# A two-layer decoder trunk on one core: the turned planes are joined on ScalarE, a token half at a time

## The chip, the core and the metric

The kernel runs on one core of one Trainium2 chip. TensorE (PE in the rows) multiplies, VectorE (DVE) and ScalarE (ACT) do the elementwise work, SyncE (SP) issues most transfers, and each engine takes its instructions strictly in the order in which they are written. The metric is the device time of one execution in microseconds (us), the median of several runs.

## What is computed

256 tokens of width 2048 pass through two layers. Each layer has one input projection, a main branch (layer 0: trailing-window means; layer 1: block attention with shared keys and values, which for 256 tokens is plain causal attention), a memory branch (4 heads over 256 memory tokens), gates, one output projection and a layer norm:

```python
for i in range(2):
    if i == 1: k, v = split(h @ w_kv_shared)              # 12 heads of 128
    branch_in, gate_b, mem_q, gate_m = split(h @ w_in[i]) # 1536, 1536, 512, 512 columns
    branch = multiscale_pool(branch_in) if i == 0 else causal_attention(branch_in, k, v)
    mem_o = memory_attention(mem_q, mem, w_mem_kv[i])
    mixed = concat(branch * silu(gate_b), mem_o * silu(gate_m))
    h = layer_norm(ALPHA * h + mixed @ w_out[i])
```

All of it is float32. Each operand of a product is held as a high and a low part, and three products are summed: high by high, high by low, low by high.

## The kernel before

**Items and blocks.** All weights come as items of 128x1024 numbers (512 KB), in a list that is walked once by `run()` (L135). One turn of its loop is called a block here. In block i the program writes, in this order: the preparation of item i+3 (`LP`: ScalarE copies `raw` into the high part `wh`, VectorE subtracts to get the low part `wl`, L73 and L74), the load of item i+4 (`LD`, on SyncE's queue), the matmuls of item i (12 of 512 columns for a projection whose tokens are stationary), and then whatever functions `later(n, fn)` has put down for this block. `raw`, `wh` and `wl` have four buffers each, so item i+3 can be prepared only when TensorE has finished item i-1. Eight items make one projection of 512 columns (`proj_n`, L209); its two token halves t=0 and t=1 end in the last item, the second half as much later as half an item takes.

**Turned projections.** Queries, keys, gates and the pooled input are wanted with channels on the partitions. `turned()` (L260) does that: ScalarE splits the result into planes of high and low 16-bit halves (L265, one instruction a token half), SyncE sends each token half as a DMA transpose (L268), and `join` (L286) puts the halves together again into 32-bit numbers, by VectorE copies of 16-bit numbers (L291) that write every second half-word. For `heads` (queries and keys) ScalarE then makes the high part (L298) and VectorE the low part one block later (L299); for `gates` (which first go through tanh, L276, and L277) and `to_pool` the joined numbers are the result. There are 9 projections for heads, 8 for gates and 3 for the pool.

**Distances.** They are counted in blocks after the last item i of the projection: sends in block i+4 (`SEND`), the join of both halves and the high part in block i+4 (`JOIN`), the low part in block i+5, for gates two blocks later for the join and one for the send. `plan(pr, a, turns, b, c)` (L471) does so for the attention of a pair of heads, counted from the last item of the query projection: scores in block `a` (6 for the first pair, 13 for the second), exponentials and division one and two later, the VectorE transposes in `turns`, the split of the probabilities in `b` and b+1, and the output, gate and split into `zT` in `c`. Nothing else sets an order: there is no scheduler.

**Order of layer 1.** Memory keys, memory values, memory queries (8 items each), memory gates, and then three groups of 32 items: keys, queries, gates, values. The first group's query projection ends 24 blocks after the memory queries. The output projection (`out_proj`, L700) ends with 16 items j8 to j23, after every second of which a kept item (one that is prepared here and multiplied after the loop) stands. `load_gb_rows` (L769) prepares four pieces of the last norm's constants (`split_rows`, L780: one ScalarE and two VectorE instructions each), in the blocks 9 to 12 after the output projection's first item.

Of the kernel before, what the change touches and what calls it, by code (L numbers as in the profile page):

```python
# [18 lines left out]
P = 128  # L19
# [23 lines left out]
LP = 3  # L43
SEND = 4
JOIN = 4
# [4 lines left out]
def trunk(ctx: ExitStack, tc: tile.TileContext, a: dict, out: bass.AP):  # L50
# [43 lines left out]
    def later(n, fn):  # L94
        events[now[0] + n].append(fn)
# [164 lines left out]
    def turned(where, then, gate=False):  # L260
# [9 lines left out]
        def done(t, acc):  # L270
# [10 lines left out]
            later(SEND + gate, lambda: send(t))  # L281
            if t == 1:
                later(JOIN + GATE * gate, lambda: then([tp.rearrange("p (h n) t -> p n h t", h=2) for tp in tps], pls[0]))
        return done

    def join(dst, tps, n0=0):  # L286

        n = dst.shape[1]
        to = dst.bitcast(U16).rearrange("p n (t h) -> p n h t", h=2)
        for t, tp in enumerate(tps):  # L290
            nc.vector.tensor_copy(to[:, :, :, t * P:(t + 1) * P], tp[:, n0:n0 + n])  # L291

    def heads(dst, where):
        def then(tps, pl):
            whole = pl.rearrange("p t h n -> p (t h n)").bitcast(F32).rearrange("p (n t) -> p n t", t=T)
            hi, lo = dst()[:, :, :T], dst()[:, :, T:]
            join(whole, tps)
            nc.scalar.activation(hi, whole, AF.Copy)  # L298
            later(1, lambda: nc.vector.tensor_sub(lo, whole, f(hi)))  # L299
        return turned(where, then)  # L300

    def gates(slots, where):
        def then(tps, pl):
            n0 = 0
            while n0 < 4:
                n = 1
                while n0 + n < 4 and slots[n0 + n] == slots[n0] + n:
                    n += 1
                join(gate[:, slots[n0]:slots[n0] + n], tps, n0)
                n0 += n  # L310
        return turned(where, then, gate=True)
# [273 lines left out]
    def mem_q_gate(layer):  # L585
# [5 lines left out]
        def go():  # L591
            plan(prs[0], 6, (9, 10, 11, 11), 12, 15)
            plan(prs[1], 13, (16, 18, 21, 23), 25, 28)
        after(go)
# [23 lines left out]
    items += [rest[0], xs[3]] + rest[1:]  # L618
    after(lambda: later(JOIN + GATE + 1, pools))

# [21 lines left out]
    def to_pool(base):  # L642
        def then(tps, pl):
            i = base
            while i < base + 4:
                n = min(3 - i % 3, base + 4 - i)
                join((U0, U1)[i // 3 % 2][:, i % 3:i % 3 + n, PAD:], tps, i - base)
                i += n
                if i % 3 == 0:
                    for j, fn in enumerate(pool_group(i // 3 - 1)):  # L650
                        n = (j + 1) // 2 + 4 * (i == 12)
                        if n:
                            later(n, fn)
                        else:
                            fn()
        return turned(in_q, then)
# [53 lines left out]
    for c in range(3):  # L710
        weave(collect(proj_n, xT, cols(a["w_in"][0], c), to_pool(4 * c)), mixes, 5)
        items += mixes
        proj_n(xT, cols(a["w_in"][0], 3 + c), gates([(4 * c + d + 4) % SLOTS for d in range(4)], in_q))
        mixes = sum((collect(pool_mix, g) for g in ((0,), (1,), (2, 3))[c]), [])
    after(lambda: later(4, load_x))

    weave(out_proj(0, range(4)), mixes, 5)

# [32 lines left out]
    for grp in range(3):  # L751
# [7 lines left out]
        def go(prs=prs, grp=grp):  # L759
            plan(prs[0], 6, (9, 10, 10, 11), 12, 19)  # L760
            plan(prs[1], 13, (16, 18, 19, 21), 23, 25)
        after(go)
# [6 lines left out]
    def load_gb_rows():  # L769
# [7 lines left out]
        for n in range(4):  # L777
            later(9 + n, lambda n=n: split_rows(f(raw)[:, n * 512:(n + 1) * 512], n))

# [174 lines left out]
```

## Time and profile before

| | us |
|---|---|
| median of 3 runs | 812.81 (812.37 to 814.1) |
| profiled execution, device time | 813.08 |
| its span, first to last instruction | 811.1 |
| TensorE busy | 798.5 (98%) |
| VectorE busy | 604.5 (75%) |
| ScalarE busy | 411.0 (51%) |

Busy time of TensorE is the union of its matmuls, each of which is drawn longer than the distance to the next one, so a pause shows in full only in the distance between two starts.

### The profile page before, as it was taken

Reading aid. Unit: us, or ns where it says so; the run is one execution under the profiler, and the core shown is the slowest. Engines: PE = TensorE matmul, PEld = TensorE weight load, DVE = VectorE, ACT = ScalarE, POOL = GpSimd, SP = SyncE. Lnnn points to the kernel's source line nnn. Section 1 sums busy time; section 2 is a strip of 40 time slices with the busy share of each in tenths; the row PEclk is TensorE's granted clock in tenths of the full one; section 3 lists DMA queues with packets and bytes.
Section 4 is the critical chain, followed back from the end, with each engine's and each line's share of the span. In section 5 each row is a group of like instructions: output and inputs, shape, how many; then the busy total and the mean of one; then the engine's idle time right before and its main releaser. Section 6 shows DMA issues by size and latency. Waiting matters only on the chain.

```text
span 811.1 us, 10158 instructions
## 1 busy us (share of the span) xinstructions
PE 798.5 (98%) x3724; PEld 664.2 (82%) x3724; DVE 604.5 (75%) x841; ACT 411.0 (51%) x523; POOL 0.2 (0%) x4
## 2 busy tenths in 40 slices
PE   9999999999999999999999998999999999999997
PEld 6888888888888888888888877888888888887786
DVE  5684699867687765687459777986589756997847
ACT  5555544655554443455455556545555655555520
POOL 0000000000000000000000000000000000000000
PEclk9999999999999999999999999999999999999999
DMA  8877777787777766686676775657765776656742
GB/s 302 289 239 245 204 187 201 187 224 219 214 228 272 252 192 192 192 279 199 197 207 176 163 215 178 204 184 208 218 187 181 200 223 197 196 183 209 268 146 104
DMA packets 110022, 169.53 MB, mean 209 GB/s; under 512 B 47632, under 2 KB 49680, under 8 KB 109712
## 3 DMA queue, kind: packets, MB, share of 16 engines
q1 hardware_dynamic: 108656, 165.70, 67.8%
q10 hardware_dynamic: 1316, 3.19, 1.1%
q8 instruction: 29, 0.48, 0.3%
q14 instruction: 21, 0.16, 0.1%
HBM read 156.28 MB, written 2.10 MB: 195 GB/s over the span
## 4 chain that ended last, share of the span: by engine, by line
PE 86%; DVE 7%; issue 2%; DMA 2%; ACT 2%; SPq 0%; DVEq 0%; ACTq 0%
PE acc L69 79%; PE s L69 3%; DVE wl L74 2%; PE o L69 2%; PE pt L69 2%; DVE p L361 1%; DMA raw<-in_w_in 1%; ACT wh L73 1%; DMA raw<-in_w_mk 1%; DVE xm L74 0%; DMA ln_g<-pl 0%; ACT ebuf L337 0%; DMA raw<-in_w_out 0%; SPq L268 0%; DVE res L488 0%
## 5 line engine op out<-in xcount | busy, mean ns | idle before, releaser
L69 PE MATMUL acc<-wh,xm 128*128 128x512 f32 x1344 | 421.4, 391 | 0.0
L74 DVE TENSOR_TENSOR wl<-raw,wh 128x1024 fp32r<-128x1024 f32 (+4 forms) x250 | 293.9, 1186 | 142.2 <-ACT wh L73 140.9
L73 ACT ACTIVATE wh<-raw 128x1024 fp32r<-128x1024 f32 (+4 forms) x250 | 254.0, 1027 | 190.9 <-PE acc L69 125.7
L69 PEld LDWEIGHTS acc<-wh,xm 128*128 128x128 f32 x1344 | 253.1, 188 | 52.3
L69 PE MATMUL acc<-wl,xm 128*128 128x512 f32 x672 | 262.6, 391 | 1.0 <-DVE wl L74 1.0
L69 PEld LDWEIGHTS acc<-wl,xm 128*128 128x128 f32 x672 | 126.7, 188 | 27.1 <-DVE wl L74 1.8
L69 PE MATMUL acc<-wh,zT 128*128 128x512 f32 x448 | 139.4, 390 | 0.0
L69 PEld LDWEIGHTS acc<-wh,zT 128*128 128x128 f32 x448 | 84.1, 188 | 17.3
L69 PE MATMUL acc<-wl,zT 128*128 128x512 f32 x224 | 87.7, 392 | 1.3 <-DVE wl L74 1.3
L69 PE MATMUL acc<-xm 128*128 128x512 f32 x288 | 66.3, 389 | 0.0
L361 DVE STREAM_TRANSPOSE p<-ebuf 32x192 f32<-32x192 f32 (+1 forms) x160 | 63.3, 396 | 2.4
L69 PEld LDWEIGHTS acc<-xm 128*128 128x128 f32 x288 | 53.9, 188 | 11.0
L74 DVE TENSOR_TENSOR xm<-raw,xm 128x1024 fp32r<-128x1024 f32 (+2 forms) x41 | 47.9, 1169 | 13.5 <-ACT xm L73 13.0
L69 PEld LDWEIGHTS acc<-wl,zT 128*128 128x128 f32 x224 | 42.1, 188 | 11.4 <-DVE wl L74 3.0
L73 ACT ACTIVATE xm<-raw 128x1024 fp32r<-128x1024 f32 (+2 forms) x41 | 41.1, 1010 | 16.6 <-DMA raw<-in_w_out 5.2
L265 ACT ACTIVATE pl<-acc 128x1024 uint16<-128x1024 uint16 x24 | 23.9, 1018 | 5.1 <-PE acc L69 4.3
L69 PE MATMUL acc<-xm,wh 128*128 128x512 f32 x64 | 24.3, 421 | 0.8 <-ACT wh L73 0.8
L69 PE MATMUL acc<-xm,zT 128*128 128x256 f32 (+1 forms) x144 | 22.6, 318 | 0.0
L337 ACT ACTIVATE ebuf<-p,nb 128x128 f32<-128x128 f32 (+1 forms) x24 | 10.7, 445 | 23.3 <-DVE nb L333 23.3
L73 ACT ACTIVATE pp<-p 128x384 fp32r<-128x384 f32 (+1 forms) x20 | 11.2, 559 | 22.1 <-DVE p L361 22.1
L69 PEld LDWEIGHTS acc<-xm,zT 128*128 128x128 f32 x144 | 20.7, 190 | 1.9
L73 ACT ACTIVATE zT<-zf 128x512 fp32r<-128x512 f32 (+1 forms) x18 | 10.5, 581 | 22.2 <-DVE zf L367 17.5
(137 smaller groups left out, 518.8 us busy)
## 6 DMA issues: line engine op xcount, KB each, us to landing
raw<-in_w_in SPq DMA_DIRECT2D x128, 512.0 KB, 4.9
raw<-in_w_out SPq DMA_DIRECT2D x64, 512.0 KB, 4.2
raw<-in_w_sk SPq DMA_DIRECT2D x24, 512.0 KB, 4.7
raw<-in_w_sv SPq DMA_DIRECT2D x24, 512.0 KB, 3.4
raw<-in_w_mv SPq DMA_DIRECT2D x14, 512.0 KB, 5.4
raw<-in_w_mk SPq DMA_DIRECT2D x12, 512.0 KB, 5.0
raw<-in_xT SPq DMA_DIRECT2D x4, 512.0 KB, 5.4
res<-in_x ACTq DMA_DIRECT2D x2, 1024.0 KB, 6.5
```

The source lines that it names most:

```text
L69: nc.tensor.matmul(o, l, r, start=start, stop=stop, **kw)
L73: nc.scalar.activation(hi, src, AF.Copy)
L74: nc.vector.tensor_sub(lo, src, f(hi))
L265: nc.scalar.activation(pls[0][:, t], src.bitcast(U16).rearrange("p (n h) -> p h n", h=2), AF.Copy)
L337: nc.scalar.activation(dst, src, AF.Exp, bias=self.nb[:, c:c + 1], scale=SCALE, accum_out=self.sm[:, c:c + 1])
L361: nc.vector.transpose(self.p[32 * g:32 * g + 32, h * self.n:(h + 1) * self.n], self.e[32 * h:32 * h + 32, g * self.n:(g + 1) * self.n])
```

## The change

The join moves from VectorE to ScalarE, as a copy by `activation`, and is done for each token half by itself: the half t in block i+4+t. For `heads` the joined half goes into the part of the `pl` tile that the same half's planes came from. To make room the sends move a block forward (`SEND` 3), the scores of all pairs and everything behind them a block back (the memory pairs' second output two: 28 to 30), the high part to block i+5 and the low part to i+6; the steps of the pool start a block after the second half's join; the woven items of the pool's mixing stand one place later, and so does the load of `x`. `split_rows` moves from 9 to 12 blocks after the output projection's first item to 31 to 34 blocks after it, which is the loop's last block and behind it.

```diff
-SEND = 4
+SEND = 3
 JOIN = 4
@@ turned
             later(SEND + gate, lambda: send(t))
+            tp = tps[t].rearrange("p (h n) x -> p n h x", h=2)
+            later(JOIN + t + GATE * gate, lambda: then(t, tp, pls[0]))
-            if t == 1:
-                later(JOIN + GATE * gate, lambda: then([...both halves...], pls[0]))
@@ join
-    def join(dst, tps, n0=0):
-        n = dst.shape[1]
-        to = dst.bitcast(U16).rearrange("p n (t h) -> p n h t", h=2)
-        for t, tp in enumerate(tps):
-            nc.vector.tensor_copy(to[:, :, :, t * P:(t + 1) * P], tp[:, n0:n0 + n])
+    def join(dst, tp, n0=0):
+        n = dst.shape[1]
+        nc.scalar.activation(dst.bitcast(U16).rearrange("p n (x h) -> p n h x", h=2), tp[:, n0:n0 + n], AF.Copy)
@@ heads
-        def then(tps, pl):
-            whole = pl.rearrange("p t h n -> p (t h n)").bitcast(F32).rearrange("p (n t) -> p n t", t=T)
-            hi, lo = dst()[:, :, :T], dst()[:, :, T:]
-            join(whole, tps)
-            nc.scalar.activation(hi, whole, AF.Copy)
-            later(1, lambda: nc.vector.tensor_sub(lo, whole, f(hi)))
+        def then(t, tp, pl):
+            whole = pl.rearrange("p t h n -> p (t h n)").bitcast(F32).rearrange("p (t n x) -> p n t x", t=2, n=4)
+            join(whole[:, :, t], tp)
+            if t == 1:
+                hi, lo = (dst()[:, :, c:c + T].rearrange("p n (t x) -> p n t x", t=2) for c in (0, T))
+                nc.scalar.activation(hi, whole, AF.Copy)
+                later(1, lambda: nc.vector.tensor_sub(lo, whole, f(hi)))
@@ gates, to_pool: the same join, for the columns t * P:(t + 1) * P alone
@@ mem_q_gate
-            plan(prs[0], 6, (9, 10, 11, 11), 12, 15)
-            plan(prs[1], 13, (16, 18, 21, 23), 25, 28)
+            plan(prs[0], 7, (10, 11, 12, 12), 13, 16)
+            plan(prs[1], 14, (17, 19, 22, 24), 26, 30)
@@ the pool
-    after(lambda: later(JOIN + GATE + 1, pools))
+    after(lambda: later(JOIN + GATE + 2, pools))
-                        n = (j + 1) // 2 + 4 * (i == 12)       (n = 0: at once)
+                        later(1 + j // 2 + 3 * (i == 12), fn)   (behind the second half)
@@ the lists: weave(..., mixes, 5) becomes 6, twice; later(4, load_x) becomes 5
@@ the three groups of layer 1
-            plan(prs[0], 6, (9, 10, 10, 11), 12, 19)
-            plan(prs[1], 13, (16, 18, 19, 21), 23, 25)
+            plan(prs[0], 7, (10, 11, 11, 12), 13, 20)
+            plan(prs[1], 14, (17, 19, 20, 22), 24, 26)
@@ load_gb_rows
-            later(9 + n, lambda n=n: split_rows(f(raw)[:, n * 512:(n + 1) * 512], n))
+            later(31 + n, lambda n=n: split_rows(f(raw)[:, n * 512:(n + 1) * 512], n))
```

What stands on the engines, at three places. First VectorE, before the change, where the memory branch of layer 1 ends and the first group's queries come in: the second memory pair's output (`zf` from `o`), its split into `zT`, the join of the queries, their low part, and the masking of the first group's scores (`p` from `s`).

```order
L74 TENSOR_TENSOR wl<-raw,wh 128x1024 x2
L367 SCALAR_TENSOR_TENSOR zf<-o,gate 128x512
L74 TENSOR_TENSOR zT<-zf,zT 128x2x256
L291 COPY pl<-ln_g 128x4x2x128 x2
L74 TENSOR_TENSOR wl<-raw,wh 128x1024
L299 TENSOR_TENSOR qq<-pl,qq 128x4x256
L74 TENSOR_TENSOR xm<-raw,xm 128x1024
```

The same place on VectorE after the change:

```order
L74 TENSOR_TENSOR wl<-raw,wh 128x1024 x2
L74 TENSOR_TENSOR xm<-raw,xm 128x1024
L366 SCALAR_TENSOR_TENSOR zf<-o,gate 128x512
L74 TENSOR_TENSOR zT<-zf,zT 128x2x256
L298 TENSOR_TENSOR qq<-pl,qq 128x4x256
L74 TENSOR_TENSOR xm<-raw,xm 128x1024
```

The join has left VectorE, and the pair's output has moved two blocks back, so that it now stands right ahead of the queries' low part, in the same block (xm is the low part of an item of the value projection).

Second ScalarE at this place, before the change (pp is the split of the second memory pair's probabilities, the joined queries are the input of L298):

```order
L73 ACTIVATE pp<-p 128x512
L73 ACTIVATE wh<-raw 128x1024 x2
L73 ACTIVATE zT<-zf 128x2x256
L298 ACTIVATE qq<-pl 128x4x256
L73 ACTIVATE wh<-raw 128x1024
L73 ACTIVATE xm<-raw 128x1024 x2
```

And after it:

```order
L73 ACTIVATE pp<-p 128x512
L73 ACTIVATE wh<-raw 128x1024
L289 ACTIVATE pl<-ln_g 128x4x2x128
L73 ACTIVATE wh<-raw 128x1024
L289 ACTIVATE pl<-ln_g 128x4x2x128
L297 ACTIVATE qq<-pl 128x4x256
L73 ACTIVATE xm<-raw 128x1024
L73 ACTIVATE zT<-zf 128x2x256
```

The two joins (L289) stand behind the preparations of two successive items, and the high part of the queries now stands ahead of the pair's `zT`, not behind it.

Third VectorE in the last part of layer 1's output projection, before the change, from the last pair's output on (kk from qq, sel and vv is a piece of the norm's constants, xm the low part of a kept item, res and stats the sums of a finished result):

```order
L467 TENSOR_TENSOR s_6000<-s_6000,zf 128x2x128
L367 SCALAR_TENSOR_TENSOR zf<-s_6000,gate 128x512
L74 TENSOR_TENSOR zT<-zf,zT 128x2x256
L74 TENSOR_TENSOR wl<-raw,wh 128x1024
L783 TENSOR_SCALAR vv<-vv,sel 5x512
L784 SCALAR_TENSOR_TENSOR kk<-qq,sel,vv 5x512
L74 TENSOR_TENSOR xm<-raw,xm 128x1024
L783 TENSOR_SCALAR vv<-vv,sel 5x512
L784 SCALAR_TENSOR_TENSOR kk<-qq,sel,vv 5x512
L74 TENSOR_TENSOR wl<-raw,wh 128x1024
```

The same part after the change:

```order
L466 TENSOR_TENSOR s_6018<-s_6018,zf 128x2x128
L366 SCALAR_TENSOR_TENSOR zf<-s_6018,gate 128x512
L74 TENSOR_TENSOR zT<-zf,zT 128x2x256
L74 TENSOR_TENSOR xm<-raw,xm 128x1024
L74 TENSOR_TENSOR wl<-raw,wh 128x1024 x2
L74 TENSOR_TENSOR xm<-raw,xm 128x1024
L74 TENSOR_TENSOR wl<-raw,wh 128x1024 x2
L487 SCALAR_TENSOR_TENSOR res<-res,acc 128x512
L488 BN_STATS stats<-res 128x6
```

The eight small instructions have gone from between the items (they now stand behind the last result), and the pair's output stands one item later.

## Rows read from the trace of the kernel before

**Rows 1.** The page's first part: of each engine the busy us, their share of the span and the instructions; and from its groups (line engine operation, tiles, form, count, us busy, mean ns of one, idle before and what ended it) the low and the high parts of the weights.

```profile
PE 798.5 (98%) x3724; PEld 664.2 (82%) x3724; DVE 604.5 (75%) x841; ACT 411.0 (51%) x523; POOL 0.2 (0%) x4
...
L74 DVE TENSOR_TENSOR wl<-raw,wh 128x1024 fp32r<-128x1024 f32 (+4 forms) x250 | 293.9, 1186 | 142.2 <-ACT wh L73 140.9
L73 ACT ACTIVATE wh<-raw 128x1024 fp32r<-128x1024 f32 (+4 forms) x250 | 254.0, 1027 | 190.9 <-PE acc L69 125.7
```

**Rows 2.** TensorE undisturbed: a piece of the chain of work that ended last (start, us, what), and the busy time by stretch for 239 us of layer 1 (stretch, its us, then busy us and instructions of PE, PEld, DVE, ACT, POOL, granted clock, DMA share and GB/s).

```profile
113.19 5.47 PE acc L69 x24
...
500.00:739.00 239.00, 239.00 (x1106) 199.54 (x1105) 189.35 (x298) 127.22 (x177) 0.00 (x0) 1.00 0.66 198
```

**Rows 3.** TensorE in order of time around its pauses at the start of layer 1's groups (start us, us, engine line operation tiles shapes xcount, and in brackets the idle time before and what ended it), and the granted clock of the stretch behind the second pause (columns as in Rows 2).

```profile
471.74 0.61 PE L69 MATMUL acc<-wh,xm 128*128 128x512 f32 x2
473.35 0.50 PE L69 MATMUL acc<-wl,xm 128*128 128x512 f32 x1 [0.99 <-DVE wl L74]
473.69 0.64 PE L69 MATMUL acc<-wh,xm 128*128 128x512 f32 x2
...
491.08 0.28 PE L69 MATMUL s<-kk,qq 128*128 128x256 f32 x1
493.77 1.39 PE L69 MATMUL s<-kk,qq 128*128 128x128 f32 x9 [2.42 <-DVE qq L299]
494.96 0.63 PE L69 MATMUL acc<-wh,xm 128*128 128x512 f32 x1
...
498.35 0.63 PE L69 MATMUL acc<-wh,xm 128*128 128x512 f32 x2
...
493.80:498.30 4.50, 4.50 (x17) 3.81 (x18) 4.08 (x8) 0.46 (x3) 0.00 (x0) 0.62 0.66 230
```

**Rows 4.** TensorE in order of time in the output projection of layer 1 (columns as in Rows 3).

```profile
743.88 0.61 PE L69 MATMUL acc<-wh,zT 128*128 128x512 f32 x2
745.18 0.50 PE L69 MATMUL acc<-wl,zT 128*128 128x512 f32 x1 [0.69 <-DVE wl L74]
...
750.30 0.61 PE L69 MATMUL acc<-wh,zT 128*128 128x512 f32 x2
750.93 0.50 PE L69 MATMUL acc<-wl,zT 128*128 128x512 f32 x1
...
756.06 0.61 PE L69 MATMUL acc<-wh,zT 128*128 128x512 f32 x2
756.97 0.50 PE L69 MATMUL acc<-wl,zT 128*128 128x512 f32 x1 [0.29 <-DVE wl L74]
...
762.08 0.61 PE L69 MATMUL acc<-wh,zT 128*128 128x512 f32 x2
763.00 0.50 PE L69 MATMUL acc<-wl,zT 128*128 128x512 f32 x1 [0.30 <-DVE wl L74]
```

**Rows 5.** The other engines ahead of the pause at 473, in order of time: the keys' planes, their transposes on SyncE's queue, the joins, the high part (columns as in Rows 3).

```profile
451.73 1.92 ACT L265 ACTIVATE pl<-acc 128x1024 uint16<-128x1024 uint16 x2
457.39 4.89 SPq L268 DMA_TRANSPOSE ln_g<-pl  x2
464.34 1.39 DVE L291 COPY pl<-ln_g 128x1024 uint16<-128x1024 uint16 x2 [2.06 <-DMA ln_g<-pl]
465.82 1.06 ACT L298 ACTIVATE kk<-pl 128x1024 fp32r<-128x1024 f32 x1 [6.18 <-DVE pl L291]
```

**Rows 6.** The engines ahead of the pause at 491, from the end of the second memory pair's output on (columns as in Rows 3).

```profile
485.61 0.40 PE L69 MATMUL acc<-wh,xm 128*128 128x512 f32 x1
485.84 0.68 DVE L367 SCALAR_TENSOR_TENSOR zf<-o,gate 128x512 f32<-128x512 f32 x1
487.22 0.69 DVE L74 TENSOR_TENSOR zT<-zf,zT 128x512 fp32r<-128x512 f32 x1 [0.70 <-ACT zT L73]
487.83 1.40 DVE L291 COPY pl<-ln_g 128x1024 uint16<-128x1024 uint16 x2
489.32 1.06 ACT L298 ACTIVATE qq<-pl 128x1024 fp32r<-128x1024 f32 x1 [2.13 <-DVE pl L291]
492.50 1.22 DVE L299 TENSOR_TENSOR qq<-pl,qq 128x1024 fp32r<-128x1024 f32 x1
```

**Rows 7.** The output projection's end: busy time by stretch (columns as in Rows 2), groups of instructions by line and form (as in Rows 1), the load of one item (KB, us from issue to landing), and in order of time the end of the last pair's output on VectorE and VectorE's idle time in the tail.

```profile
739.00:764.00 25.00, 23.71 (x101) 18.34 (x100) 24.46 (x30) 15.58 (x18) 0.00 (x0) 1.00 0.69 224
...
L784 DVE SCALAR_TENSOR_TENSOR kk<-qq,sel,vv 5x512 fp32r<-5x512 f32 x4 | 3.0, 738 | 0.1
...
L783 DVE TENSOR_SCALAR vv<-vv,sel 5x512 f32<-5x512 f32 x4 | 1.9, 469 | 0.0
...
raw<-in_w_out SPq DMA_DIRECT2D x13, 512.0 KB, 3.4
...
738.34 0.69 DVE L74 TENSOR_TENSOR zT<-zf,zT 128x512 fp32r<-128x512 f32 x1 [0.70 <-ACT zT L73]
...
790.35 0.69 DVE L830 SCALAR_TENSOR_TENSOR res<-res,acc 128x512 f32<-128x512 f32 x1 [7.66 <-PE acc L69]
```

**Rows 8.** What is moved and what it is like: the planes by line and form (columns as in Rows 1), all joins of the run by busy time (stretch, us, DVE busy and instructions, clock, DMA share, GB/s), and the transposes' time from issue to landing.

```profile
L265 ACT ACTIVATE pl<-acc 128x1024 uint16<-128x1024 uint16 x24 | 23.9, 1018 | 5.1 <-PE acc L69 4.3 <-DVE kk L299 0.9
...
0.00:811.10 811.10, 29.60 (x50) 1.00 0.69 209
...
DMA to landing us min/median/max: 3.2/4.7/6.4
```

More of the change, by code (lines that the diff above doesn't have):

```diff
@@ L281, in done, with heads, then @@
             later(SEND + gate, lambda: send(t))
-            if t == 1:
-                later(JOIN + GATE * gate, lambda: then([tp.rearrange("p (h n) t -> p n h t", h=2) for tp in tps], pls[0]))
-        return done
-    def join(dst, tps, n0=0):
-        n = dst.shape[1]
-        to = dst.bitcast(U16).rearrange("p n (t h) -> p n h t", h=2)
-        for t, tp in enumerate(tps):
-            nc.vector.tensor_copy(to[:, :, :, t * P:(t + 1) * P], tp[:, n0:n0 + n])
-    def heads(dst, where):
-        def then(tps, pl):
-            whole = pl.rearrange("p t h n -> p (t h n)").bitcast(F32).rearrange("p (n t) -> p n t", t=T)
-            hi, lo = dst()[:, :, :T], dst()[:, :, T:]
-            join(whole, tps)
-            nc.scalar.activation(hi, whole, AF.Copy)
-            later(1, lambda: nc.vector.tensor_sub(lo, whole, f(hi)))
+            tp = tps[t].rearrange("p (h n) x -> p n h x", h=2)
+            later(JOIN + t + GATE * gate, lambda: then(t, tp, pls[0]))
+        return done
+    def join(dst, tp, n0=0):
+        n = dst.shape[1]
+        nc.scalar.activation(dst.bitcast(U16).rearrange("p n (x h) -> p n h x", h=2), tp[:, n0:n0 + n], AF.Copy)
+    def heads(dst, where):
+        def then(t, tp, pl):
+            whole = pl.rearrange("p t h n -> p (t h n)").bitcast(F32).rearrange("p (t n x) -> p n t x", t=2, n=4)
+            join(whole[:, :, t], tp)
+            if t == 1:
+                hi, lo = (dst()[:, :, c:c + T].rearrange("p n (t x) -> p n t x", t=2) for c in (0, T))
+                nc.scalar.activation(hi, whole, AF.Copy)
+                later(1, lambda: nc.vector.tensor_sub(lo, whole, f(hi)))
         return turned(where, then)
     def gates(slots, where):
-        def then(tps, pl):
+        def then(t, tp, pl):
             n0 = 0
@@ L308, in then @@
                     n += 1
-                join(gate[:, slots[n0]:slots[n0] + n], tps, n0)
+                join(gate[:, slots[n0]:slots[n0] + n, t * P:(t + 1) * P], tp, n0)
                 n0 += n
@@ L642, in to_pool, with then @@
     def to_pool(base):
-        def then(tps, pl):
+        def then(t, tp, pl):
             i = base
@@ L646, in then @@
                 n = min(3 - i % 3, base + 4 - i)
-                join((U0, U1)[i // 3 % 2][:, i % 3:i % 3 + n, PAD:], tps, i - base)
+                join((U0, U1)[i // 3 % 2][:, i % 3:i % 3 + n, PAD + t * P:PAD + (t + 1) * P], tp, i - base)
                 i += n
-                if i % 3 == 0:
+                if t == 1 and i % 3 == 0:
                     for j, fn in enumerate(pool_group(i // 3 - 1)):
[L651 to L655, printed above, removed]
+                        later(1 + j // 2 + 3 * (i == 12), fn)
         return turned(in_q, then)
@@ L710, in trunk @@
     for c in range(3):
-        weave(collect(proj_n, xT, cols(a["w_in"][0], c), to_pool(4 * c)), mixes, 5)
+        weave(collect(proj_n, xT, cols(a["w_in"][0], c), to_pool(4 * c)), mixes, 6)
         items += mixes
@@ L714, in trunk @@
         mixes = sum((collect(pool_mix, g) for g in ((0,), (1,), (2, 3))[c]), [])
-    after(lambda: later(4, load_x))
-    weave(out_proj(0, range(4)), mixes, 5)
+    after(lambda: later(5, load_x))
+    weave(out_proj(0, range(4)), mixes, 6)
     gbs = {}
```

## The prediction

> **What bounds the kernel.** I read the page's busy times first: TensorE is busy 98% of the span, VectorE 75%, ScalarE 51% [rows 1]. So I look for what is not TensorE's own work: places where the distance between the starts of two matmuls is longer than usual. Undisturbed, 24 matmuls take 5.47 us, 0.23 each, so an item of 12 takes 2.74 us, and from 500 to 739 us TensorE does not pause at all [rows 2]. The views in order of time then show where it does, and what ended each pause:
>
> - At 473: the two matmuls from 471.74 start at 471.74 and 471.97, the next one not at 472.20 but at 473.35, and the one behind it 0.34 instead of 0.23 later: 1.15 + 0.11 = 1.26 us, ended by VectorE's low part of the weights [rows 3].
> - At 491: 2.69 us between two score matmuls that otherwise start 0.12 apart, ended by the low part of the queries: 2.57 us. Behind it the granted clock is 0.62 on average for 4.5 us, so part of it is at the lower level of 1.2 GHz, and eight distances take 3.39 us instead of 1.82: another 1.57 us [rows 3]. The shorter pause at 473 was not followed by this: the next distance but one is again the usual one.
> - In the last output projection, at 745.18, 750.93, 756.97 and 763.00, all waiting for VectorE's low part: the starts come 0.84, 0.17, 0.45 and 0.46 us late, and with 0.1 more behind each as at 473, 2.3 us [rows 3, 4].
>
> Together 7.7 us. The ramp at the start and the tail are the same in both kernels, so this is nearly all that an order of work can win. What follows asks of each pause if it goes, and what is late next.
>
> **The join itself.** 50 VectorE copies of 29.6 us in all go [rows 8]; they hold 40 times 1024 numbers a partition. On ScalarE no such copy is in the trace. The nearest row is the planes' copy, the same count and type, with every second half-word on the reading side where the join has it on the writing side: 1.02 us [rows 8]. I take that, d = 1.02, so some 41 us and a little for the smaller pieces. Bounds: 0.70, VectorE's time for the same copy [rows 5], and twice the planes' copy, 2.04, if writing apart were slow. ScalarE goes from 411 to some 453 us, 56% of the span; VectorE from 604.5 to 575 [rows 1].
>
> None of that is on the path unless it is late for a score or for weights. For weights there is room: the four buffers let the preparation run three items ahead. For the scores I walk a query projection whose last item ends at T, with 2.74 us a block. ScalarE: the high part of item i+7 can start when item i+3 is done, T+8.2, and ends at 9.3; first join 10.3; high part of item i+8 (not before 10.96) 12.0; second join 13.0; high part of the queries (1.06) 14.1; of item i+9 15.1. VectorE: low part of item i+9 16.3, of the queries (1.22) 17.5 [rows 1, 6]. TensorE reaches these scores at T+19.2 and wants the low part 0.12 later. So there are 1.8 us to spare, and with d = 2.04 still 0.3; from d = 2.2 (the end is then 14.9 + 2d) the scores wait.
>
> Do the halves land in time? Before, the planes were ready at 453.65, but the transposes began at 457.39, since they stood behind the load of item i+8, which waits for VectorE to empty its buffer; VectorE could go on with both halves at 464.34, 6.95 us after the start [rows 5]. One block forward they stand behind the load of item i+7, whose buffer is emptied before T, and wait for their planes alone, ready at about T+1.0. Landed by about T+8, they are ahead of both joins (9.3 and 12.0); even the 10.7 us from planes to join before would give T+11.7. Behind the transposes on SyncE's queue is now the load of item i+8: it goes out at about T+6 (4.89 us for the pair [rows 5]) instead of T+4, lands 3.4 to 5 us later [rows 7], and ScalarE wants it at T+11: no cost; if it were 2 us late, the three items' lead would cover it.
>
> **The pause at 473** came from this: ScalarE stood 6.18 us behind the high part of the keys, which waited for VectorE's join, which waited 2.06 us for the transposes [rows 5]. In that time no weights were prepared. The transposes now start 3 us earlier, and VectorE has 2 x 0.70 us less for the keys and as much for the gates. I take the whole 1.26 us as won; between 0.5 and 1.26.
>
> **The pause at 491.** Here the change trades one order for another. Before, the output of the second memory pair and the join of the queries stood in the same block; the end of the output's matmuls (485.61) was followed by 7 us on VectorE and ScalarE until the low part began at 492.50, against two items on TensorE, 5.5 us [rows 6]. Now the output is two blocks later, so in the block in which the low part is written, and ahead of it; join and high part are done by then. Let the output end at C. VectorE's gate begins at C+0.23 and the low part in zT is done at C+2.30 (485.84 and 487.22 plus 0.69, against 485.61); the next instruction began at C+2.22 [rows 6]. That is now the queries' low part, 1.22 us, done at C+3.44. TensorE does one item, 2.74, and wants it 0.12 later, at C+2.86, and the last semaphore takes 0.05: a pause of 0.63 us is left of 2.57. The pause at 473 was longer, 0.99 idle, and the clock stayed up, so I take the slow stretch as gone. Won: 1.94 + 1.57 = 3.5 us.
>
> **The last output projection.** From 739 to 764 VectorE was busy 24.46 of 25.0 us [rows 7]: it alone sets the pace. The four pieces of constants are 4 x (0.74 + 0.47) = 4.8 us of it [rows 7]. Put behind the loop, they lie in the 7.66 us in which VectorE waits for the tail's first result [rows 7]; with that cover gone they would cost up to 4.8, but 2.8 are to spare. Against that, the last pair's output is one item later, so TensorE is one item closer to the unprepared weights when ScalarE and VectorE come free. Walked from the end of that output's matmuls (736.03), with 3.0 us until its zT (738.34 + 0.69 [rows 7]), 1.05 and 1.2 us an item, a load 3.3 to 4 us after its buffer is free, 2.7 us for each pair of sums: the low parts of items j12, j16 and j18 are ready at 5.6, 16.1 and 22.2, wanted at 5.7, 16.7 and 22.15. Margins of that size mean small pauses: I take 0.3 us of the 2.3 as left, between 0 and 1.5. Won: 2.0.
>
> The other moves I cost at nothing. The scores' later blocks keep their distances, and exponentials that now stand behind the tanh of the gates are 1.1 us later with three items' lead. The woven mixing leaves one item between the last mix and its use; its chain is some 2.3 us long against 3.4. The pool's steps come later but have eight blocks until their use.
>
> **The sum.** 1.26 + 3.5 + 2.0 = 6.8 us. From the profiled execution, 813.08, that gives 806.3; the median shown is 0.27 lower, so 806.0.
>
> A rule speaks against the move. VectorE does this copy in 0.70 us, ScalarE one like it in 1.02 [rows 5, 8]. The Trainium skill, page "ScalarE: Activation LUTs", section "Rules for kernel authors", says plain elementwise work belongs on VectorE, which is up to three times as fast. By that alone the change adds 11 us of engine time; by the rows the time of an engine that is not awaited is free, and VectorE is the one awaited in every pause. The rule wins only if ScalarE becomes late, which is the fourth rival.
>
> **The rivals.**
> 1. *The loads bound the last output projection.* With VectorE freed, the four landing buffers may set the pace: 3.4 us to land, 1.05 and 1.2 to use is 5.7 to 6.5 us for four items, 1.4 to 1.6 each against 1.83 wanted; for it speaks that ends of loads bunch. The 2.0 us stay lost: 808.0.
> 2. *The first group's scores still wait long.* If the low part finds one more item's low part ahead of it, or the high part late, the pause is again 2.4 us with the slow stretch behind: 806.0 + 1.94 + 1.57 = 809.5.
> 3. *The change does not do what it says:* pauses go from the named places and turn up at others, because ScalarE's order now ties weights to transposes. All is given back: 811.5 to 814, no change.
> 4. *Slower: the join on ScalarE is slow,* because it writes two bytes in every four. It decides from d = 2.9: then five query projections wait 1.4 us each and eat the gain. At d = 3.6, three and a half times the planes' copy, each waits 14.9 + 7.2 - 19.3 = 2.8 us, with a slow stretch of 1.57 behind: 5 x 4.4 = 22 us, 828. No row of either engine shows a copy of this count so long.
>
> **How the numbers follow.** Forecast 0.60 (805 to 807.5); rival 1 0.15, rival 2 0.10, rival 3 0.08, rival 4 0.07. A measurement of this kernel can tell 0.2%, 1.6 us, from no change. The first three cases are faster: 0.85, and a little of rival 3: 0.86; same 0.08; slower 0.06. The range takes in the first three cases: from all 7.7 us won (805.1, less 0.4 for the runs' spread) to rival 2: 804.7 to 809.7.
>
> **What would show it.** Right: joins of 1.0 us on ScalarE; TensorE without a pause at 473; one pause of about 0.6 us at the first group's scores and a granted clock of 1.0 behind it; the constants in VectorE's wait in the tail; at most 1 us lost from 735 to 763. Wrong: joins over 2.2 us; ScalarE idle behind transposes; scores of every group ended by the queries' low part; ScalarE waiting for loads while TensorE pauses.

## The result and the profile after

The changed kernel takes 808.23 us (median of 4 runs, 807.75 to 808.74) against 812.59 for the one before (4 runs, 811.8 to 814.1): a ratio of 0.9944, 95% interval 0.9927 to 0.9961. It is faster by 4.4 us, where 6.8 were forecast. The time lies inside the predicted range, 2.2 us above the predicted one. The profiled execution took 808.74 us, its span 807.0.

The page's first part and the two groups of weights, which answer to [rows 1]:

```profile
PE 795.8 (99%) x3724; PEld 662.7 (82%) x3724; DVE 576.9 (71%) x791; ACT 459.9 (57%) x573; POOL 0.2 (0%) x4
...
L74 DVE TENSOR_TENSOR wl<-raw,wh 128x1024 fp32r<-128x1024 f32 (+2 forms) x250 | 293.9, 1186 | 169.4 <-ACT wh L73 168.1
L73 ACT ACTIVATE wh<-raw 128x1024 fp32r<-128x1024 f32 (+2 forms) x250 | 252.8, 1026 | 166.9 <-PE acc L69 99.8
```

VectorE lost 27.6 us of work and ScalarE gained 48.9; TensorE's 3724 matmuls are the same. All that counts is where TensorE pauses. To compare places I take, of each run's trace, the starts of neighbouring matmuls and add up what each distance has over the usual one (0.228 us behind a matmul of 512 columns, as [rows 2] gives it). This is the time lost by stretch, in us of one profiled execution each (distances less than some 0.09 us over the usual one are left out):

| kernel | span | layer 0 (75 to 345) | 382 to 480 | first scores, 480 to 505 | 505 to 700 | last output projection |
|---|---|---|---|---|---|---|
| before | 811.1 | 0 | 1.27 | 4.25 | 0.40 | 2.38 |
| changed | 807.0 | 1.14 | 0 | 0.80 | 0 | 1.64 |

The sum falls from 8.30 to 3.58, so by 4.7. The start (before 65 us, the same code) came 0.87 later in this execution, which leaves 3.8. The spans differ by 4.1; the 0.3 between the two lies in distances too small to be counted, not in the tail: from the last pause in the output projection (763.00 [rows 4] and 758.81) to the tail's first sums (790.35 [rows 7] and 786.16) both kernels take 27.35 us.

**At 473** nothing is left: TensorE in order of time (start, us, what), where [rows 3] had 1.26 us.

```profile
471.60 0.62 PE L69 MATMUL acc<-wh,xm 128*128 128x512 f32 x2
472.05 0.39 PE L69 MATMUL acc<-wl,xm 128*128 128x512 f32 x1
...
472.96 0.62 PE L69 MATMUL acc<-wh,xm 128*128 128x512 f32 x2
```

The chain ahead of it, answering to [rows 5] (ScalarE, and SyncE's queue):

```profile
453.74 1.94 ACT L265 ACTIVATE pl<-acc 128x1024 uint16<-128x1024 uint16 x2
455.61 3.45 SPq L268 DMA_TRANSPOSE ln_g<-pl  x2
461.48 1.36 ACT L289 ACTIVATE pl<-ln_g 128x1024 uint16<-128x1024 uint16 x1
...
465.97 1.36 ACT L289 ACTIVATE pl<-ln_g 128x1024 uint16<-128x1024 uint16 x1
```

The planes are done at 455.68 and the transposes are sent in the same moment; before, they stood 3.74 us behind a load. Neither join has an idle time before it.

**At the first group's scores** one short pause is left. TensorE there, then the granted clock behind it (stretch, its us, busy us and instructions of PE, PEld, DVE, ACT, POOL, clock, DMA share, GB/s):

```profile
494.36 0.28 PE L69 MATMUL s<-kk,qq 128*128 128x256 f32 x1
495.18 1.32 PE L69 MATMUL s<-kk,qq 128*128 128x128 f32 x9 [0.54 <-DVE qq L298]
```

```profile
495.00:500.00 5.00, 4.82 (x26) 4.17 (x27) 4.66 (x9) 1.47 (x4) 0.00 (x0) 1.00 0.33 105
```

495.18 - 494.36 - 0.13 = 0.69 us, and 0.1 behind it, where there were 2.57 and 1.57 [rows 3]. The clock stays at 1.00, the upper level. VectorE and ScalarE ahead of it, answering to [rows 6]:

```profile
488.73 1.06 ACT L297 ACTIVATE qq<-pl 128x1024 fp32r<-128x1024 f32 x1
...
491.91 0.68 DVE L366 SCALAR_TENSOR_TENSOR zf<-o,gate 128x512 f32<-128x512 f32 x1
...
493.30 0.69 DVE L74 TENSOR_TENSOR zT<-zf,zT 128x512 fp32r<-128x512 f32 x1 [0.70 <-ACT zT L73]
...
493.91 1.22 DVE L298 TENSOR_TENSOR qq<-pl,qq 128x1024 fp32r<-128x1024 f32 x1
```

The high part of the queries starts 5 us ahead of the low part (488.73 and 493.91); the low part stands behind the pair's output on VectorE, starts 2.00 us after that output's gate and ends at 495.13, 0.05 before the scores go on.

**In the last output projection** three pauses are left of four. They are those of [rows 4] at 745, 757 and 763, at 741.02 (0.21 us with the matmul behind it instead of 0.94), 752.77 (0.85, some 0.55 before) and 758.81 (0.58, about as before); the one at 751 is gone. TensorE, then ScalarE and VectorE, then the busy times of the stretch:

```profile
740.47 0.61 PE L69 MATMUL acc<-wh,zT 128*128 128x512 f32 x2
741.02 0.50 PE L69 MATMUL acc<-wl,zT 128*128 128x512 f32 x1
...
752.77 0.50 PE L69 MATMUL acc<-wl,zT 128*128 128x512 f32 x1 [0.58 <-DVE wl L74]
...
758.81 0.50 PE L69 MATMUL acc<-wl,zT 128*128 128x512 f32 x1 [0.30 <-DVE wl L74]
```

```profile
743.23 1.06 ACT L73 ACTIVATE wh<-raw 128x1024 fp32r<-128x1024 f32 x1 [1.81 <-DMA raw<-in_w_out]
744.32 1.23 DVE L74 TENSOR_TENSOR wl<-raw,wh 128x1024 fp32r<-128x1024 f32 x1 [1.08 <-ACT wh L73]
745.50 1.06 ACT L73 ACTIVATE wh<-raw 128x1024 fp32r<-128x1024 f32 x1 [1.22 <-DMA raw<-in_w_out]
746.59 1.22 DVE L74 TENSOR_TENSOR wl<-raw,wh 128x1024 fp32r<-128x1024 f32 x1 [1.05 <-ACT wh L73]
747.49 1.06 ACT L73 ACTIVATE xm<-raw 128x1024 fp32r<-128x1024 f32 x1 [0.93 <-DMA raw<-in_w_out]
747.74 0.68 DVE L487 SCALAR_TENSOR_TENSOR res<-res,acc 128x512 f32<-128x512 f32 x1
...
750.38 1.20 DVE L74 TENSOR_TENSOR xm<-raw,xm 128x1024 fp32r<-128x1024 f32 x1
```

```profile
740.00:764.00 24.00, 23.12 (x100) 18.19 (x99) 19.98 (x21) 12.71 (x13) 0.00 (x0) 1.00 0.79 262
```

VectorE is no longer busy throughout: 19.98 of the 24 us from 740 to 764, where [rows 7] had 24.46 of 25. It waits twice for ScalarE, which waits for loads. Then four sums keep it from the weights for 2.6 us (747.74 to 750.38), and the pause at 752.77 follows. The constants lie in the tail, four pairs of instructions from 776.61 to 781.36 (the first one is shown), and VectorE's wait for the tail's first result is 3.00 us instead of the 7.66 of [rows 7]:

```profile
776.61 0.46 DVE L778 TENSOR_SCALAR vv<-vv,sel 5x512 f32<-5x512 f32 x1
...
786.16 0.69 DVE L825 SCALAR_TENSOR_TENSOR res<-res,acc 128x512 f32<-128x512 f32 x1 [3.00 <-PE acc L69]
```

**New pauses in layer 0**, where the kernel before had none: 0.51 us at 154 and 0.64 at 266.6. First the engines ahead of 154, then those ahead of 266.6:

```profile
145.65 0.95 DVE L637 TENSOR_TENSOR res<-res 128x768 f32<-128x768 f32 x1
146.63 0.84 ACT L73 ACTIVATE zT<-res 128x768 fp32r<-128x768 f32 x1 [5.57 <-DVE res L637]
...
154.02 0.50 PE L69 MATMUL acc<-wl,xm 128*128 128x512 f32 x1 [0.23 <-DVE wl L74]
...
264.22 1.80 ACT L73 ACTIVATE wh<-raw 128x1024 fp32r<-128x1024 f32 x2 [5.05 <-DMA raw<-in_w_out]
...
266.59 0.50 PE L69 MATMUL acc<-wl,zT 128*128 128x512 f32 x1 [0.36 <-DVE wl L74]
```

ScalarE stands for 5.57 us behind the pool's last step on VectorE, a subtraction, because the split of its result is next in ScalarE's order; no weights are prepared meanwhile. In the kernel before it stood there for 2.76 us, and TensorE did not pause.

**The join itself**, all calls of its line of one kind (ns least/median/most):

```profile
L289 ACT ACTIVATE pl<-ln_g x14: 1353/1356/1363, 413.5 to 672.0; 128x1024 uint16<-128x1024 uint16 x14
L289 ACT ACTIVATE res<-qq x12: 470/768/1067, 132.9 to 229.9; 128x768 uint16<-128x768 uint16 x4, 128x256 uint16<-128x256 uint16 x4, 128x512 uint16<-128x512 uint16 x4
```

### The profile page after: what moved, and what is told of

Read it like the earlier page. It is cut to its first block, busy times and chain, and to the rows that moved or that the text cites. A ratio compares the mean times of both kernels' runs of the same rounds, so it can differ in the third digit from the quotient of the medians.

```text
span 807.0 us, 10124 instructions
## 1 busy us (share of the span) xinstructions
PE 795.8 (99%) x3724; PEld 662.7 (82%) x3724; DVE 576.9 (71%) x791; ACT 459.9 (57%) x573; POOL 0.2 (0%) x4
## 4 chain that ended last, share of the span: by engine, by line
PE 70%; DVE 14%; DMA 7%; ACT 5%; issue 4%; SPq 0%; DVEq 0%; ACTq 0%
PE acc L69 64%; DVE wl L74 6%; DMA raw<-in_w_in 3%; DVE p L360 3%; DMA raw<-in_w_out 3%; ACT wh L73 2%; PE s L69 2%; PE o L69 2%; PE pt L69 1%; DVE xm L74 1%; DMA raw<-in_w_mk 1%; DVE res L628 1%; ACT xm L73 0%; ACT ebuf L336 0%; DVE pp L74 0%
## 5 line engine op out<-in xcount | busy, mean ns | idle before, releaser
L74 DVE TENSOR_TENSOR wl<-raw,wh 128x1024 fp32r<-128x1024 f32 (+2 forms) x250 | 293.9, 1186 | 169.4 <-ACT wh L73 168.1
L73 ACT ACTIVATE wh<-raw 128x1024 fp32r<-128x1024 f32 (+2 forms) x250 | 252.8, 1026 | 166.9 <-PE acc L69 99.8
L289 ACT ACTIVATE pl<-ln_g 128x1024 uint16<-128x1024 uint16 x14 | 19.0, 1357 | 0.0
```

Of the source, the lines that this page charges most:

```text
L73: nc.scalar.activation(hi, src, AF.Copy)
L74: nc.vector.tensor_sub(lo, src, f(hi))
L289: nc.scalar.activation(dst.bitcast(U16).rearrange("p n (x h) -> p n h x", h=2), tp[:, n0:n0 + n], AF.Copy)
```

## The experiments

The theory: the order won, not the engine; what remains is one output ahead of a low part, the pool's steps, and the last output projection. Rivals: the loads set that projection's pace whatever stands there, and the join's engine made part of the gain. Losses by stretch of all kernels, as in the table above (us):

| kernel | span | layer 0 | 382 to 480 | first scores | 505 to 700 | last output projection |
|---|---|---|---|---|---|---|
| e4_join_dve | 804.9 | 0.63 | 0 | 1.57 | 0 | 1.74 |
| e3_send3 | 808.9 | 0 | 0 | 4.20 | 0.41 | 2.40 |
| e1_rows_late | 808.6 | 0.09 | 1.84 | 4.12 | 0.40 | 0.69 |
| e2_rows_early | 807.6 | 1.54 | 0 | 0.71 | 0 | 3.76 |
| e5_x4 | 805.4 | 1.84 | 0 | 0.71 | 0.41 | 1.59 |
| e6_split_later | 804.2 | 0 | 0 | 0.71 | 0 | 1.75 |
| e7_c31 | 804.5 | 0.11 | 0 | 0 | 0 | 1.93 |
| e8_last_c25 | 804.2 | 1.37 | 0 | 0.71 | 0 | 0.83 |
| e9_three | 803.1 | 0 | 0 | 0 | 0 | 0.69 |
| e10_three_sums | 803.3 | 0 | 0 | 0 | 0.95 | 0.67 |
| e11_changed_again | 804.1 | 0.11 | 0 | 0.71 | 0 | 1.52 |
| e12_three_dve | 804.8 | 0 | 0 | 0.20 | 0.77 | 1.20 |

Each row is one execution, and the same code scatters. From 505 to 700 seven of the nine kernels with the changed order and the join on ScalarE lost nothing, e5 0.41 and e10 0.95, though their edits lie elsewhere. TensorE's 300th matmul, up to which its work is the same in all fourteen kernels, starts between 65.92 and 68.55 us, so the start alone moves a time by up to 2.6 us.

The first four ran on one chip, beside 18 runs of the kernel before (median 812.22 us).

**e4_join_dve**: the changed kernel with the join back on VectorE, all of the order kept.

```diff
-        nc.scalar.activation(dst.bitcast(U16).rearrange("p n (x h) -> p n h x", h=2), tp[:, n0:n0 + n], AF.Copy)
+        nc.vector.tensor_copy(dst.bitcast(U16).rearrange("p n (x h) -> p n h x", h=2), tp[:, n0:n0 + n])
```

> The changed kernel with the join back on VectorE, in the new places (half by half, sends three blocks back, scores seven). Theory 'order': the two pauses went because transposes, joins and scores have more blocks between them; TensorE again has no pause at 473, one of 0.6 to 0.8 us at the first group's scores, and the time is within 1 us of the changed kernel's 808.2. Theory 'engine': the 29.6 us taken off VectorE did it; the pause at 473 (over 0.8 us) is back and the time is 810.5 or more.

Measured: 808.32 us (806.64 to 809.67, 4 runs), 0.9948 [0.9929, 0.9966]. VectorE is back at 604.5 us busy, ScalarE at 411.4, and the time is the changed kernel's: the engine is worth less than these runs can tell, and nothing is lost at 473. But the pause at the first scores, expected at 0.6 to 0.8, is 1.47 us, with the clock still up (PE, then the stretch's busy times):

```profile
491.39 0.28 PE L69 MATMUL s<-kk,qq 128*128 128x256 f32 x1
492.98 1.32 PE L69 MATMUL s<-kk,qq 128*128 128x128 f32 x9 [1.31 <-DVE qq L298]
```

```profile
495.00:500.00 5.00, 5.00 (x23) 4.13 (x23) 4.20 (x8) 3.51 (x11) 0.00 (x0) 1.00 0.42 157
```

Here the engine does count. First e4: the join of the queries' second half and the gate of the pair's output, on VectorE. Then the changed kernel: the same join on ScalarE and the high part of the weights ahead of it.

```profile
485.75 0.75 DVE L289 COPY pl<-ln_g 128x1024 uint16<-128x1024 uint16 x1
...
489.71 0.68 DVE L366 SCALAR_TENSOR_TENSOR zf<-o,gate 128x512 f32<-128x512 f32 x1
```

```profile
486.38 1.06 ACT L73 ACTIVATE wh<-raw 128x1024 fp32r<-128x1024 f32 x1 [1.78 <-DMA raw<-in_w_in]
487.34 1.36 ACT L289 ACTIVATE pl<-ln_g 128x1024 uint16<-128x1024 uint16 x1
```

On ScalarE the join follows the high part of the weights at once and ends 1.26 us after it (487.44 and 488.70). On VectorE it also waits for their low part, which stands between, and ends 1.93 us after the high part (484.57 and 486.50). The queries' high part, an item of the value projection and the pair's gate hang on it in turn: in e4 the gate starts 1.07 us after the output's matmuls (488.64), in the changed kernel 0.29 us after them (491.62). The difference, 0.78 us, is that of the two pauses.

**e3_send3**: the kernel before, with the transposes one block earlier and nothing else.

```diff
-SEND = 4
+SEND = 3
```

> The kernel before with SEND 3 alone. If the pause at 473 came from transposes that started late behind a load, and the one at 491 from the memory pair's output ahead of the join, then the first goes and the second stays at 2.4 us or more: 1.2 us faster than before, 811.4. Rival: both hung on the late transposes; both go, 5 us faster, 807.5. Second rival: neither goes, since the join's place is what counts, 812.6.

Measured: 810.47 us (808.75 to 813.93, 10 runs), 0.9985 [0.997, 1.0]. The pause at 473 is gone by this alone (first two lines: the starts are 0.45 us apart, two usual distances). The one at the scores stays whole, 2.55 us, and the clock falls behind it:

```profile
470.94 0.61 PE L69 MATMUL acc<-wh,xm 128*128 128x512 f32 x2
471.39 0.39 PE L69 MATMUL acc<-wl,xm 128*128 128x512 f32 x1
...
491.61 1.32 PE L69 MATMUL s<-kk,qq 128*128 128x128 f32 x9 [2.39 <-DVE qq L299]
```

```profile
495.00:500.00 5.00, 5.00 (x20) 4.04 (x19) 3.22 (x5) 3.41 (x10) 0.00 (x0) 0.85 0.33 119
```

So 473 hung on transposes behind a load, and the scores did not: what the change has besides, and e4 keeps, is the later output and the later scores, which were not tried one by one. The trace shows this; the time alone would not, since its interval reaches 1.0.

**e1_rows_late** is the kernel before with the constants alone moved; **e2_rows_early** is the changed kernel with the constants where they were.

```diff
@@ e1_rows_late (e2_rows_early: the reverse)
-            later(9 + n, lambda n=n: split_rows(f(raw)[:, n * 512:(n + 1) * 512], n))
+            later(31 + n, lambda n=n: split_rows(f(raw)[:, n * 512:(n + 1) * 512], n))
```

> The kernel before with the norm's constants behind the loop alone. If VectorE alone set the pace of the last output projection, the lost 2.3 us there fall to 0.4 or less: 2.0 us faster, 810.6. If the loads set it, 1.5 us or so stay lost, with VectorE idle while ScalarE waits for loads: 0.8 us faster, 811.8.

> The changed kernel with the norm's constants back in blocks 9 to 12. If VectorE sets the pace, 4.8 us more of work on it make the 1.6 us lost in the last output projection 3 us or more: 809.7 or more. If the loads do, they stay under 2.2: under 808.8.

Measured: e1 810.4 us (809.88 to 812.89, 8 runs), 0.9981 [0.9969, 0.9993], with 0.69 us left in the last output projection of 2.38. e2 809.32 us (808.03 to 809.89, 5 runs), 0.996 [0.9946, 0.9975], with 3.76 left there: one pause of 2.08 us, and the lower clock behind it.

```profile
739.00 0.64 PE L69 MATMUL acc<-wh,zT 128*128 128x512 f32 x2
741.54 0.50 PE L69 MATMUL acc<-wl,zT 128*128 128x512 f32 x1 [1.89 <-DVE wl L74]
```

```profile
742.00:747.00 5.00, 5.00 (x17) 3.96 (x16) 4.96 (x6) 2.14 (x3) 0.00 (x0) 0.66 0.58 211
```

Moving the constants is worth 1.7 us in the old order and 2.1 in the new one (3.76 - 1.64). The 0.69 left in e1 lie between the 0.4 of the one theory and the 1.5 of the other; e2's 3.76 is what VectorE's pace gives. But e1, with the pair's output in its old block, has 0.95 less left than the changed kernel: a first sign that the later output costs there.

The next four are single runs of the changed kernel with one edit each, beside one run of the kernel before at 812.77 us. Times of one run say little at this size; the losses by stretch are what they were made for.

**e5_x4**: the load of the next input one block earlier, for the pause at 266.

```diff
-    after(lambda: later(5, load_x))
+    after(lambda: later(4, load_x))
```

> The changed kernel with the 2 MB load of x one block earlier, where it was. If the pause at 266 comes from that load running into the loads of the weights (ScalarE then waited 5.05 us for one), the 0.64 us go. If it comes from the joins on ScalarE ahead of the weights there, they stay. All other pauses stay as in the changed kernel.

Measured: 807.18 us. There is no pause at 266, but e2, e6, e7 and e11, with that load where the change put it, have none there either. So the edit shows nothing: the 0.64 us came in one execution (e8 has 0.18 at this place), behind a weight load on which ScalarE waited 5.05 us. That wait alone does not make it, since e4's ScalarE waited 5.20 us for the same load without a pause; the cause stays open.

**e6_split_later**: the split of the pool's result, the last of its steps, one block later.

```diff
-                    for j, fn in enumerate(pool_group(i // 3 - 1)):
-                        later(1 + j // 2 + 3 * (i == 12), fn)
+                    steps = pool_group(i // 3 - 1)
+                    for j, fn in enumerate(steps):
+                        later(1 + j // 2 + 3 * (i == 12) + (fn is steps[-1]), fn)
```

> The changed kernel with the pool's last step (the split into zT, ScalarE's only part in it) one block later. If the pause at 154 comes from ScalarE standing 5.6 us behind VectorE's subtraction with no weights prepared meanwhile, the 0.51 us go. If VectorE's own work (transposes and pool steps in the same blocks) is too much there, 0.4 us or more stay.

Measured: 806.02 us, and no loss in layer 0 at all. ScalarE has the same split after 0.27 us of waiting instead of 5.57:

```profile
144.72 0.85 ACT L73 ACTIVATE zT<-res 128x768 fp32r<-128x768 f32 x1 [0.27 <-DVE res L637]
```

The seven executions with the pool as the change has it lost between 0.11 and 1.84 us in layer 0 (the changed kernel's first one with the 0.64 at 266 among it), five of them 0.6 or more; the four with this edit (e6, e9, e10, e12) lost none. ScalarE waited 5.0 to 5.8 us in all seven, so the same wait costs more or less by execution.

**e7_c31**: the second memory pair's output behind the block of the queries' low part.

```diff
-            plan(prs[1], 14, (17, 19, 22, 24), 26, 30)
+            plan(prs[1], 14, (17, 19, 22, 24), 26, 31)
```

> The changed kernel with the second memory pair's output one block later (31 for 30), behind the queries' low part. If that output ahead of the low part in the same block is what leaves 0.7 us at the first group's scores, the pause falls to 0.1 or less. If the joins or the high part on ScalarE are late, 0.5 us or more stay.

Measured: 806.24 us, no pause at the scores: they follow the output's matmuls without a gap.

```profile
490.86 1.60 PE L69 MATMUL o<-pp,vv 128*128 128x256 f32 x12
492.29 1.34 PE L69 MATMUL s<-kk,qq 128*128 128x256 f32 x10
```

**e8_last_c25**: for the last group alone, the second pair's output one block earlier, as it was before the change.

```diff
-            plan(prs[1], 14, (17, 19, 20, 22), 24, 26)
+            plan(prs[1], 14, *(((17, 18, 20, 21), 23, 25) if grp == 2 else ((17, 19, 20, 22), 24, 26)))
```

> The changed kernel with the last group's second pair one block earlier from the second transpose on (18, 20, 21, split 23, output 25). If the output one item later is what lost the last output projection its margin, the lost 1.64 us there fall to 0.7, what is left in the kernel before with the constants alone moved. If the loads set the pace, 1.4 or more stay.

Measured: 806.01 us, 0.83 left in the last output projection instead of 1.64. The last pause, that of 763 in [rows 4], remains with 0.57, and 0.25 at 750.04.

The last four ran on one chip, beside 11 runs of the kernel before (median 812.35 us). **e9_three** has the edits of e6, e7 and e8 together; **e11_changed_again** is the changed kernel without an edit; **e12_three_dve** is e9 with e4's join on VectorE.

> The changed kernel with three moves together: the pool's split one block later, the second memory pair's output in block 31, the last group's second pair's output in block 25. Each took its pause away alone, and they touch different places: no pause at 154 and at the scores, 0.8 us left in the last output projection, 1.1 in all behind the start against 4.2 in the changed kernel's profile: 2 to 3 us faster than the changed kernel, a ratio of 0.991 to 0.993. If a pause moves on when it is taken away, the ratio stays at 0.9945.

> The changed kernel as it is, beside the three on the same chip, for its ratio and to see which of its pauses come again: the one at the scores (0.7) and the two in the last output projection (1.6) do, if they hang on the order; the one at 266, which no other kernel with the same code there showed, does not, if a load of the weights that came late once is its cause.

> The three moves with the join on VectorE. Theory 'order' (the engine of the join is worth nothing once no output stands ahead of the low part): within 1 us of the kernel with the three moves, pauses within 0.5 us. Theory 'engine': VectorE is short of time in the groups of layer 1 again, 1.5 us or more of new pauses there.

Measured: e9 804.76 us (804.45 to 805.54, 4 runs), 0.9913 [0.9896, 0.9931]; e11 807.46 (805.86 to 809.09, 6 runs), 0.9949 [0.993, 0.9967]; e12 805.45 (804.33 to 807.01, 6 runs), 0.9922 [0.9906, 0.9939]. e9 beats both kernels: its slowest run is below the fastest of the changed one. In time the join's engine once more shows no difference beyond the intervals. The profiled executions differ: e12 lost 2.17 us in the table's stretches and e9 0.69, where at most 0.5 more was expected if the order alone counts, and 1.5 more in the groups if the engine does. Of it 0.77 us is a pause at the second group's scores, at 585.30, ended by the queries' low part; but e5 (0.42) and e10 (0.34) paused there too with the join on ScalarE, so one execution of e12 does not tell the engine from scatter. In e9 TensorE does not pause from 382 to 740. The one pause left, at 755.06, with VectorE and ScalarE ahead of it:

```profile
750.02 0.68 DVE L487 SCALAR_TENSOR_TENSOR res<-res,acc 128x512 f32<-128x512 f32 x1
...
752.66 1.21 DVE L74 TENSOR_TENSOR xm<-raw,xm 128x1024 fp32r<-128x1024 f32 x1
753.72 1.06 ACT L73 ACTIVATE wh<-raw 128x1024 fp32r<-128x1024 f32 x1 [1.49 <-DMA raw<-in_w_out]
753.79 2.36 DVE L74 TENSOR_TENSOR wl<-raw,wh 128x1024 fp32r<-128x1024 f32 x2
...
755.06 0.50 PE L69 MATMUL acc<-wl,zT 128*128 128x512 f32 x1 [0.33 <-DVE wl L74]
```

VectorE works without a break from the sums at 750.02 to the low part that TensorE wants, while ScalarE waits for loads.

**e10_three_sums**: e9 with the sums of the second result two blocks later, to take them from the low parts.

```diff
-    def to_residual(n):
+    def to_residual(n, wait=0):
         def done(t, acc):
+            if wait:
+                later(wait, lambda: sums(t, acc))
+            else:
+                sums(t, acc)
+
+        def sums(t, acc):
             r = res[:, t, n * 512:(n + 1) * 512]
...
-            return collect(proj_n, zT, w, to_residual(n), (*FIRST[layer], *(kb for kb in range(8) if kb not in FIRST[layer])))
+            return collect(proj_n, zT, w, to_residual(n, 2 * (layer and n == 1)), (*FIRST[layer], *(kb for kb in range(8) if kb not in FIRST[layer])))
```

> The same with the residual sums of the second result of the last output projection two blocks later, behind the next two items' low parts. If the 2.7 us of sums ahead of those low parts leave the 0.6 us at 756, the loss there falls to 0.3 or less and the time by 0.5 us more; if the loads set the pace, it stays at 0.8.

Measured: 805.02 us (804.37 to 805.78, 4 runs), 0.9916 [0.9898, 0.9933]. The pause behind the moved sums is gone, but one of nearly the same size, 0.56 of the 0.67 us, has come at 749.57, behind the first result's four sums, where e9 had none. So the place of one set of sums does not settle it. Whether faster loads would was not tried; this remainder of 0.7 us stays unattributed between sums and loads.

## Why the prediction was right, and where it missed

**Right, in its mechanism.** *The pause at 473*: 1.26 us forecast as won, 1.27 won; the cause was the transposes behind a load, as e3 shows alone. *The pause at 491*: forecast 0.63 us left and the clock up; 0.69 left, with 0.1 behind it, at a clock of 1.00. The walk held in its steps: the queries' low part began 2.00 us behind the pair's gate, forecast 1.99 (C+2.22 less C+0.23). e7 shows that this output makes all of the rest: without it ahead of the low part the scores do not wait. *The constants*: they lie in the tail's wait, which fell from 7.66 to 3.00 us, with no cost there.

**Mis-sized: what is left in the last output projection.** I took "0.3 us of the 2.3 as left, between 0 and 1.5"; it was 1.64 (1.52 in e11). The walk gave margins of -0.05 to 0.6 us from loads that land 3.3 to 4 us after their buffer is free; ScalarE now waited 1.81, 1.22 and 0.93 us for loads in a row, VectorE stood for 1.08 and 1.05 behind it, and so had no lead when the four sums came. (ScalarE had waited for loads before the change as well: 1.02, 1.36 and 1.21 us from 745 to 751.) Two things make the 1.64: the pair's output one block later costs about 0.8 (e8: 0.83 left), and 0.67 to 0.83 stay where it stands one block earlier (e1, e8, e9, e10; 1.20 in e12, with the join on VectorE). So the first rival, the loads, was true in part: ScalarE did wait for them, but at most 0.7 of its 2.0 us can be theirs alone, since e9 has 0.69 left with the loads as they are. Of the signs named, "at most 1 us lost from 735 to 763" did not come, and ScalarE waited for loads ahead of TensorE's pauses, hardly during them. That the time, 808.23, is almost this rival's 808.0 is chance: of what is missing to 806.0 about half came elsewhere, at the start and in layer 0.

**Wrong: "the other moves I cost at nothing", of which the pool's.** I argued that its steps "come later but have eight blocks until their use". Their use on TensorE was not the question: the split is an instruction in ScalarE's order, and ScalarE waited up to 5.57 us there with weights behind it. That cost 0.51 us in the profiled execution, and e6 removed it. The second pause in layer 0 (0.64 us) came in this size in this execution alone and is not explained.

**The join's size.** Taken at 1.02 us, measured 1.36, a third more: ScalarE is busy for 459.9 us, forecast 453; VectorE 576.9, forecast 575. It stayed below the 2.2 us from which the scores would wait, so it cost nothing, as the working had it (e7, e9: no pause there). VectorE's 0.70 us was half of a pair that overlaps; one copy took 0.75, before and in e4. The rule that plain elementwise work belongs on VectorE (the Trainium skill, "ScalarE: Activation LUTs", "Rules for kernel authors"; its row names relu, max, min, add and mul, and gives the factor of three for bf16) agrees with the engines' times here, 1.36 us against 0.75 in e4. It does not settle the kernel's: e4 and e12 are within the intervals of their twins, and at e4's scores the quicker copy, behind the low part of the weights, was done later.

**The sum again.** The span was forecast at 811.1 - 6.8 = 804.3 and came to 807.0, so 2.7 more: the last output projection 1.3, layer 0 1.1, the first scores 0.2, the start 0.9; less 0.4 for a small pause between 505 and 700 that I had not counted and that went, less 0.2 for losses of the kernel before that I had taken slightly low, and less 0.2 in distances too small to be placed. The tail is the same. The start is the same code and differs by up to 2.6 us between executions, so part of the miss is chance.

## What to carry to other kernels

When an instruction is moved later on an engine that works in order, ask not only when its result is used but what stands behind it on that engine while it waits for its input: the pool's split and the pair's output each cost here what they held up. Moving work to another engine buys time only where something awaited stands behind it: the join's engine is not told apart in the time here, and counts for 0.8 us at the one pause that hangs on it (e4). Moving the send of a slow transfer ahead of a load (e3), and an output behind the operand that is due first (e7), took pauses away. Work that is taken off a bound engine pays only up to the next limit, so walk the loads, and not the engine alone, through the stretch.

## What the runs showed of the hardware

- A ScalarE copy of 1024 half-words a partition that writes every second one took 1.36 us; the planes' copy, which reads every second one, 1.02 to 1.04 in the same run. By size it took 0.47, 0.77, 1.07 and 1.36 us for 256, 512, 768 and 1024: some 0.30 us for each 256 more. VectorE's copy of 1024, which writes every second one too, took 0.75 us before the change and in e4.
- A pause of 1.47 us (e4) left TensorE's clock at the upper level of 2.4 GHz. Behind pauses of 2.08 us (e2) and 2.55 (e3) the granted clock was 0.66 (742 to 747) and 0.85 (495 to 500) on average, so part of the time at 1.2 GHz; that added about 1.6 us to each of these pauses.
